# ConvFFN up projection as seven half-size products per pair of tiles, on one Trainium2 core

## The chip, the cores and the metric

The kernel runs on one core of a Trainium2 chip. The metric is the device time of one execution in microseconds (us): 802.35 us in the median of three runs (802.0 to 802.36). The engines of the core are called PE (TensorE, matrix multiply; PEld is its weight load), DVE (VectorE), ACT (ScalarE), POOL (GpSimd) and SP (SyncE, which here only issues DMA transfers). Each engine takes its instructions in the order in which they stand in its own queue, and waits on semaphores of the others.

## What is computed

One layer of a decoder trunk on a sequence of 512 tokens with 1024 features. A mixer of two gated branches comes first, then the ConvFFN, then a gated embedding and a last norm. The change concerns the ConvFFN, cut to its core here (D_FF is 2816):

```python
h = rmsnorm(x, ffn_norm)
up = h @ w_up                              # [512,1024] @ [1024, 5632]
conv = conv_b + sum(conv_w[k] * up_pad[:, k:k+T] for k in range(3))   # causal, width 3
a, b = conv[..., :2816], conv[..., 2816:]
x = x + (gelu(a) * b) @ w_down             # [512,2816] @ [2816, 1024]
```

All data is float32. The kernel splits every operand exactly into two float32r parts, high and low, and makes one product of three matmuls: high by high, high by low, low by high.

## The kernel before

Features lie on partitions, tokens on the free axis, in tiles of 128 x 512. `mm3` (L107 to L111) is one product of a 128 x 128 weight block with a 128 x 512 operand in three matmuls. `proj8` runs it over the eight k tiles of one output tile (24 matmuls into one PSUM bank).

Weights come as chunks of 128 x 1024 (512 KB). `chunk` (L53 to L61) issues one DMA on SP into `raw` (3 buffers), ACT casts `whi<-raw` (L59), DVE subtracts `wlo<-raw,whi` (L60). `take` hands out the chunks in a planned order and has each loaded two chunks ahead of its use.

The ConvFFN runs 22 times over a pair of f tiles, tile 2i (for a) and 2i+1 (for b). Per tile: `proj8`, then `conv` (L393 on): DVE multiplies the bank by the norm row R (L396), ACT scales (L398), DVE adds the two shifted terms (L399, L401). Then ACT takes gelu (L408), DVE multiplies a by b (L410), and `split` (L153, L154) stores the pair's h tile in two parts. After all 22 pairs the down projection runs over eight output tiles, 66 matmuls each, and `residual` adds each to x. The order of instructions on every engine is set by the tile framework's scheduler from program order and waits for buffers.

Of the kernel before, what the change touches and what calls it, by code (L numbers as in the profile page):

```python
# [36 lines left out]
def trunk(ctx, tc, xT, pT, wsT, par, bsp, w_p0, w_p1, w_v, w_u, w_ga, w_gb, w_pl,  # L37
# [15 lines left out]
    def chunk(src, cols=CW, keep=False, first=False):  # L53
        raw = wp.tile([P, CW], F32, tag="raw", name="raw", bufs=3)
# [39 lines left out]
    for f in range(KD):  # L94
        plan(w_o[f].rearrange(flat))
    for i in range(2 * KF):
        plan(w_up[i].rearrange(flat))
    DK = [(k0, min(8, KF - k0)) for k0 in range(0, KF, 8)]
    for f in range(KD):
        for k0, n in DK:  # L100
            plan(w_dn[f, :, k0:k0 + n, :].rearrange(flat), n * P)
# [91 lines left out]
    class Norm:
        """Sums squares of feature-major tiles; gives 1/rms by token and broadcast over partitions."""
# [19 lines left out]
        def row(self, r):  # L214
            """r[token] on every partition: ones times its diagonal blocks, in two exact parts."""
            rb = pst.tile([P, T], F32, tag="st", name="rb")
            dh = tmp.tile([P, PAD + T], F32R, tag="pad", name="dh", bufs=4)
            dl = tmp.tile([P, PAD + T], F32R, tag="pad", name="dl", bufs=4)
            for b in range(NT):
                c = slice(b * P, (b + 1) * P)  # L220
                V.tensor_scalar_mul(dh[:, c], ident, r[:, b:b + 1])
# [4 lines left out]
            return rb
# [18 lines left out]
    src, cols, kw = todo.pop(0)  # L245
    ready.append(chunk(src, cols, **kw))
# [123 lines left out]
    def residual(f, o, cg, nm=None):  # L370
        """x[f] += o; the next operand, and the sum of squares, with it."""
        xn = x[f]
        V.tensor_tensor(xn, o, xn, op=ALU.add)
        b = xgp.tile([P, 2, T], F32R, tag="xg", name="xg")
        split_into(b, xn, col(cg, f))
        if nm is not None:
            nm.add(xn)
        return b

# [1 line left out]
    nm = Norm()  # L381
    xg = [residual(f, proj8(m), C_FFN, nm) for f in range(KD)]

# [1 line left out]
    def up():  # L385
        return proj8(xg)

    up_o = [up()]
    r_tok = nm.token()
    up_o.append(up())  # L390
    R = nm.row_sb(r_tok)

    def conv(i):  # L393
        o = up_o[i] if i < len(up_o) else up()
        z = work("up")
        V.tensor_tensor(z, o, R, op=ALU.mult)  # L396
# [8 lines left out]
    h = []
    for i in range(KF):
        a = conv(2 * i)
        S.activation(a, a, AF.Gelu)  # L408
        b = conv(2 * i + 1)
        V.tensor_tensor(a, a, b, op=ALU.mult)  # L410
        h.append(split(a))
# [153 lines left out]
```

## Time and profile before

| | before |
|---|---|
| median of the runs | 802.35 us |
| profiled execution, span | 799.6 us |
| PE busy / DVE busy / ACT busy / POOL busy | 790.9 / 448.1 / 309.6 / 14.1 us |
| ConvFFN up stretch (373.27 to 614.08) | 240.8 us |
| down stretch (614.08 to 733.77) | 119.7 us |

The page gives the profiled execution as its span alone; the runs lie 2.75 us above it at the median, and that difference is taken as the time around the span. A matmul's duration in the trace holds its pipeline delay, so what one costs in a row of many is the distance from one start to the next.

### The profile page before, as it was taken

How to read it: one execution, taken by the hardware profiler on the slowest of the kernel's cores; microseconds unless marked ns; L12 is line 12 of the kernel's file. 1: busy time of each engine (PE TensorE's matmuls, PEld its weight loads, DVE VectorE, ACT ScalarE, POOL GpSimd, SP SyncE). 2: the span in 40 equal slices, each digit the busy share in tenths (PEclk: the TensorE clock that was granted, in tenths of full speed). 3: DMA queues.
4: the chain of work that ended last, by engine and by line, in shares of the span. 5: the costliest groups of instructions: out<-in, count | busy, mean ns of one | idle time of the engine just before them, and what ended most of it. 6: DMA issues, size and time to landing. Idle time of an engine off the chain costs nothing.

```text
span 799.6 us, 9000 instructions
## 1 busy us (share of the span) xinstructions
PE 790.9 (99%) x3566; PEld 657.6 (82%) x3566; DVE 448.1 (56%) x606; ACT 309.6 (39%) x421; POOL 14.1 (2%) x72
## 2 busy tenths in 40 slices
PE   9999999999999999999999999999999999999996
PEld 7888888888888888888888888888888888888885
DVE  7696353333665444555777777777777333235345
ACT  5235542223333232343444444444444222224534
POOL 0200000000000000000000000000000000000010
PEclk9999999999999999999999999999999999999999
DMA  7522322322222222223233233223233333325111
GB/s 251 202 82 78 131 93 92 105 94 91 81 93 90 90 96 105 100 86 105 80 106 105 82 103 105 85 101 106 83 101 118 98 94 100 98 99 173 64 53 54
DMA packets 24666, 81.44 MB, mean 102 GB/s; under 512 B 2864, under 2 KB 2992, under 8 KB 24624
## 3 DMA queue, kind: packets, MB, share of 16 engines
q1 hardware_dynamic: 23616, 78.65, 29.0%
q10 hardware_dynamic: 1008, 2.21, 0.9%
q8 instruction: 28, 0.46, 0.2%
q14 instruction: 14, 0.11, 0.0%
HBM read 78.75 MB, written 2.10 MB: 101 GB/s over the span
## 4 chain that ended last, share of the span: by engine, by line
PE 98%; DMA 0%; ACT 0%; DVE 0%; POOLq 0%; issue 0%; SPq 0%; ACTq 0%
PE mm L109 32%; PE mm L110 32%; PE mm L111 32%; PE mm L352 1%; PE mm L467 0%; DMA x<-in_xT 0%; PE ss L211 0%; ACT xg L156 0%; ACT ple L494 0%; POOLq L561 0%; ACT mm L487 0%; PE rb L224 0%; PE rb L225 0%; ACT mm L484 0%; DVE ple L485 0%
## 5 line engine op out<-in xcount | busy, mean ns | idle before, releaser
L59 ACT CAST whi<-raw 128x1024 fp32r<-128x1024 f32 (+1 forms) x141 | 146.0, 1038 | 312.7 <-PE mm L110 201.4
L109 PE MATMUL mm<-xg,whi 128*128 128x512 f32 x608 | 237.1, 391 | 0.5 <-ACT xg L156 0.5
L111 PE MATMUL mm<-xg,wlo 128*128 128x512 f32 x608 | 236.6, 389 | 0.0
L110 PE MATMUL mm<-xg,whi 128*128 128x512 f32 x608 | 236.6, 389 | 0.0
L60 DVE TENSOR_TENSOR wlo<-raw,whi 128x1024 fp32r<-128x1024 f32 (+1 forms) x148 | 174.4, 1180 | 105.4 <-ACT whi L59 103.2
L111 PE MATMUL mm<-blk,wlo 128*128 128x512 f32 x384 | 149.4, 389 | 0.0
L109 PE MATMUL mm<-blk,whi 128*128 128x512 f32 x384 | 149.4, 389 | 0.0
L110 PE MATMUL mm<-blk,whi 128*128 128x512 f32 x384 | 149.4, 389 | 0.0
L109 PEld LDWEIGHTS mm<-xg,whi 128*128 128x128 f32 x608 | 114.1, 188 | 24.0 <-ACT xg L156 0.7
L111 PEld LDWEIGHTS mm<-xg,wlo 128*128 128x128 f32 x608 | 114.2, 188 | 23.8
L110 PEld LDWEIGHTS mm<-xg,whi 128*128 128x128 f32 x608 | 114.1, 188 | 23.4
L111 PEld LDWEIGHTS mm<-blk,wlo 128*128 128x128 f32 x384 | 72.1, 188 | 15.0
L109 PEld LDWEIGHTS mm<-blk,whi 128*128 128x128 f32 x384 | 72.1, 188 | 15.0
L110 PEld LDWEIGHTS mm<-blk,whi 128*128 128x128 f32 x384 | 72.1, 188 | 14.9
L109 PE MATMUL mm<-whi,xg 128*128 128x512 f32 (+1 forms) x136 | 51.6, 379 | 0.0
L396 DVE TENSOR_TENSOR up<-mm,R 128x512 f32<-128x512 f32 x44 | 30.2, 687 | 38.1 <-PE mm L111 38.1
L111 PE MATMUL mm<-whi,xg 128*128 128x512 f32 (+1 forms) x136 | 51.2, 377 | 0.0
L110 PE MATMUL mm<-wlo,xg 128*128 128x512 f32 (+1 forms) x136 | 51.2, 377 | 0.0
L398 ACT ACTIVATE cc<-up,pr 128x512 f32<-128x512 f32 x44 | 35.7, 813 | 1.7 <-DVE up L396 1.4
L153 ACT CAST blk<-cc 128x512 fp32r<-128x512 f32 x22 | 13.7, 621 | 56.9 <-DVE cc L410 56.9
L332 DVE TENSOR_TENSOR gt<-mm,R 128x512 f32<-128x512 f32 x16 | 11.1, 692 | 42.5 <-PE mm L111 42.5
L401 DVE SCALAR_TENSOR_TENSOR cc<-up,pr,cc 128x510 f32<-128x510 f32 x44 | 33.0, 750 | 1.6
(104 smaller groups left out, 503.7 us busy)
## 6 DMA issues: line engine op xcount, KB each, us to landing
raw<-in_w_up SPq DMA_DIRECT2D x44, 512.0 KB, 3.2
raw<-in_w_dn SPq DMA_DIRECT2D x16, 512.0 KB, 3.5
raw<-in_w_v SPq DMA_DIRECT2D x8, 512.0 KB, 3.3
raw<-in_w_ga SPq DMA_DIRECT2D x8, 512.0 KB, 3.3
raw<-in_w_a SPq DMA_DIRECT2D x8, 512.0 KB, 3.2
raw<-in_w_u SPq DMA_DIRECT2D x8, 512.0 KB, 3.2
raw<-in_w_gb SPq DMA_DIRECT2D x8, 512.0 KB, 3.3
raw<-in_w_b SPq DMA_DIRECT2D x8, 512.0 KB, 3.2
```

The costliest lines, as they stand in the source:

```text
L59: (V.tensor_copy if first else S.copy)(hi[:, :cols], raw[:, :cols])
L60: V.tensor_tensor(lo[:, :cols], raw[:, :cols], hi[:, :cols].bitcast(F32), op=ALU.subtract)
L109: PE.matmul(o, wh, ah, start=first, stop=False)
L110: PE.matmul(o, wh, al, start=False, stop=False)
L111: PE.matmul(o, wl, ah, start=False, stop=last)
L153: S.copy(b[:, 0, :], src)
L332: V.tensor_tensor(gt, o, Rb, op=ALU.mult)
L352: PE.matmul(mx[:, n * P:(n + 1) * P], vt[n][:, f * P:(f + 1) * P], wsm[:, f, :], start=True, stop=True)
L396: V.tensor_tensor(z, o, R, op=ALU.mult)
L398: S.activation(cc, z, AF.Identity, scale=col(C_CW, 3 * i + 2), bias=col(C_CB, i))
L401: V.scalar_tensor_tensor(cc[:, 2:], z[:, :T - 2], col(C_CW, 3 * i), cc[:, 2:], op0=ALU.mult, op1=ALU.add)
```

## The change

Two output tiles of a pair, two halves of k (four k tiles each) and two halves of the tokens (256 each) make a 2 x 2 by 2 x 2 block product, which is formed by seven half-size products instead of eight (Strassen, Winograd's form). A product is now 4 k tiles x 3 matmuls of 128 x 256, and a pair has 84 of them in place of 48 of 128 x 512.

The operand sides (x times the norm's gain, and sums and differences of its halves) are made once, in `sides`, while the mixer's output projection runs. The weight sides are sums made per pair, in `sums`: `w1` is the plain chunk of the first tile; `ta` and `tb` hold the sums. Each of `ta` and `tb` is filled by one plain DMA from SP (256 KB), then one DMA issued by POOL that adds to what has landed, then one POOL addition (L108, L115); only then can ACT and DVE split it. The last chunk is the half `raw` that `two` loaded. So a pair splits 3.5 chunks in place of 2.

The down projection is cut into 22 steps of 24 matmuls: groups of four h tiles for two output tiles each (the last two steps: two h tiles, four output tiles), with each partial sum added to x. Seventeen steps stand between the products of pairs 5 to 21, five after the last pair.

The diff without its comment lines, cut to the core:

```diff
+NBLK = 26
+WB = 5
+HK = KD // 2
+FAHEAD = 3
+GS = 4
-    wp = ctx.enter_context(tc.tile_pool(name="wp", bufs=3))
+    wp = ctx.enter_context(tc.tile_pool(name="wp", bufs=WB))
-    xgp = ctx.enter_context(tc.tile_pool(name="xgp", bufs=8))
-    blk = ctx.enter_context(tc.tile_pool(name="blk", bufs=22))
+    blk = ctx.enter_context(tc.tile_pool(name="blk", bufs=NBLK))
...
+    def sums(f1, f2):
+        got = {}
+        top, bot = slice(0, HK), slice(HK, KD)
+        half = HK * P
+        flat = "p k f -> p (k f)"
+        def one():
+            got["1"] = raw_tile()
+            nc.sync.dma_start(got["1"], f1.rearrange(flat))
+            return parts(got["1"])
+        def two():
+            t = got["a"] = blk.tile([P, CW], F32, tag="blk", name="ta")
+            nc.sync.dma_start(t[:, :half], f1[:, top].rearrange(flat))
+            nc.gpsimd.dma_start(t[:, :half], f2[:, top].rearrange(flat), accum_op=ALU.add)
+            r = got["2"] = raw_tile()
+            nc.sync.dma_start(r[:, :half], f2[:, bot].rearrange(flat))
+            G.tensor_tensor(t[:, half:], t[:, :half], r[:, :half], op=ALU.add)
+            return parts(t)
+        def three():
+            t = blk.tile([P, CW], F32, tag="blk", name="tb")
+            nc.sync.dma_start(t[:, :half], f2[:, top].rearrange(flat))
+            nc.gpsimd.dma_start(t[:, :half], f2[:, bot].rearrange(flat), accum_op=ALU.add)
+            G.tensor_tensor(t[:, half:], got["a"][:, half:], got["1"][:, half:], op=ALU.add)
+            return parts(t)
+        return [one, two, three, lambda: parts(got["2"], half)]
...
+    def product(o, w, j, c, first=False):
+        for k in range(HK):
+            wh, wl = wslice(w, j * HK + k)
+            a = side(c, k)
+            for n, (p, q) in enumerate(((wh, a[:, 0]), (wh, a[:, 1]), (wl, a[:, 0]))):
+                PE.matmul(o, p, q, start=first and k == 0 and n == 0, stop=k == HK - 1 and n == 2, skip_group_check=True)
+        def begin(self):
+            self.w1 = take(FAHEAD)
+            self.p1 = bank()[:, :H]
+            self.b = seeded[self.i % 2][:, :H]
+            product(self.p1, self.w1, 0, 0, first=True)
+            S.copy(self.b, self.p1)
+        def middle(self):
+            wa = take(FAHEAD)
+            self.c = bank()[:, :H]
+            product(self.c, wa, 0, 3, first=True)
+            product(self.b, wa, 1, 4)
+            self.u = work("u").rearrange("p (a t) -> p a t", a=2)
+            S.copy(self.u[:, 0], self.b)
+            product(self.p1, self.w1, 1, 1)
+            V.tensor_tensor(self.z1[:, :H], self.p1, R[:, :H], op=ALU.mult)
+            self.wb = take(FAHEAD)
+            product(self.b, self.wb, 0, 5)
+            S.copy(self.u[:, 1], self.b)
+            V.tensor_tensor(self.z2[:, H:], self.c, self.u[:, 1], op=ALU.subtract)
+        def end(self):
+            product(self.b, self.wb, 1, 2)
+            V.tensor_tensor(self.z1[:, H:], self.b, R[:, H:], op=ALU.mult)
+            product(self.c, take(FAHEAD), 0, 6)
+            V.tensor_tensor(self.z2[:, :H], self.c, self.u[:, 0], op=ALU.subtract)
+            V.tensor_tensor(self.z2, self.z2, R, op=ALU.mult)
...
+    for i in range(KF):
+        pair.middle()
+        if order[i]:
+            down(order[i])
+        after = None
+        if i + 1 < KF:
+            after = Pair(i + 1)
+            after.begin()
+        h.append(pair.end())
+        pair = after
+    for step in steps:
+        down(step)
```

How the order of instructions moves is shown at two queues and, for one of them, the engine that it feeds. The SP queue of the kernel before, in the middle of the up stretch, holds one load per chunk, each waiting for DVE to have read the buffer's last content:

```order
L58 DMA raw_3471<-in_w_up 128x1024 [waits DMAHW2_49,DVE_49]
L58 DMA raw_3512<-in_w_up 128x1024 [waits DMAHW3_49,DVE_49]
L58 DMA raw_3550<-in_w_up 128x1024 [waits DMAHW4_49,DVE_49]
L58 DMA raw_3591<-in_w_up 128x1024 [waits DMAHW5_49,DVE_49]
L58 DMA raw_3629<-in_w_up 128x1024 [waits DMAHW6_49,DVE_49]
```

The SP queue of the changed kernel for one pair (pair 7) with a step of the down projection. `raw_3910` takes the buffer of `raw_3665`, the last chunk of pair 6 (a row of the DVE queue below); `ta_3835` and `tb_3875` are pair 7's sums:

```order
L99 DMA raw_3771<-in_w_up 128x1024 [waits DMAHW4_49,Pool_49]
L107 DMA raw_3838<-in_w_up 128x512 [waits DMAHW6_49,DMAHW1_49,DVE_49]
L62 DMA raw_3910<-in_w_dn 128x512 [waits DMAHW5_49,DVE_49,Activation_49]
L104 DMA ta_3835<-in_w_up 128x512 [waits DMASW0_49]
L113 DMA tb_3875<-in_w_up 128x512 [waits DMASW1_49]
L62 DMA raw_3910<-in_w_dn 128x512 [waits DMAHW7_49]
L99 DMA raw_3944<-in_w_up 128x1024 [waits DMAHW2_49,DMAHW0_49,Pool_49]
```

One load per chunk has become six issues per pair, and the loads of the sums stand behind a load that waits for DVE's last subtraction of the pair before. The POOL queue, which has no instruction in the up stretch before but one small one of the norm, now holds for each pair, here 6 and 7:

```order
L105 DMA ta_3662<-in_w_up 128x512 [waits DMAHW7_49,DMASW5_49,DVE_49]
L114 DMA tb_3702<-in_w_up 128x512 [waits DMAHW0_49,DVE_49]
L108 TENSOR_TENSOR ta_3662<-ta_3662,raw_3665 128x512 [waits DMAHW5_49,DMASW4_49]
L115 TENSOR_TENSOR tb_3702<-ta_3662,raw_3598 128x512 [waits DMAHW4_49,Pool_49]
L105 DMA ta_3835<-in_w_up 128x512 [waits DMAHW5_49,DVE_49]
L114 DMA tb_3875<-in_w_up 128x512 [waits DMASW7_49,DMAHW6_49,DMASW1_49,DVE_49]
L108 TENSOR_TENSOR ta_3835<-ta_3835,raw_3838 128x512 [waits DMAHW3_49,DMASW6_49]
L115 TENSOR_TENSOR tb_3875<-ta_3835,raw_3771 128x512 [waits DMAHW2_49,Pool_49]
```

Each is new: two adding transfers and two additions per pair. The DVE queue of the kernel before, for about one pair:

```order
L396 TENSOR_TENSOR up_3780<-mm_3755,R_2861 128x512 [waits PE_49]
L60 TENSOR_TENSOR wlo_3789<-raw_3787,whi_3788 128x1024 [waits DMAHW5_49,Activation_49]
L399 SCALAR_TENSOR_TENSOR cc_3782<-up_3780,pr_82,cc_3782 128x511 [waits Activation_49]
L401 SCALAR_TENSOR_TENSOR cc_3782<-up_3780,pr_82,cc_3782 128x510 [waits DVE_49]
L396 TENSOR_TENSOR up_3818<-mm_3793,R_2861 128x512 [waits PE_49]
L60 TENSOR_TENSOR wlo_3830<-raw_3828,whi_3829 128x1024 [waits DMAHW6_49,Activation_49]
L399 SCALAR_TENSOR_TENSOR cc_3820<-up_3818,pr_82,cc_3820 128x511 [waits Activation_49]
```

The DVE queue of the changed kernel, from the subtraction of pair 6's `ta` to that of its last chunk (`raw_3665`):

```order
L74 TENSOR_TENSOR wlo_3669<-ta_3662,whi_3668 128x1024 [waits DMASW4_49,Activation_49]
L74 TENSOR_TENSOR wlo_3707<-tb_3702,whi_3706 128x1024 [waits DMASW5_49,Activation_49]
L74 TENSOR_TENSOR wlo_3741<-raw_3737,whi_3740 128x1024 [waits DMAHW6_49,DMAHW1_49,Activation_49]
L520 TENSOR_TENSOR z2_3528<-z2_3528,R_2905 128x512 [waits DVE_49]
L532 SCALAR_TENSOR_TENSOR cc_3758<-z1_3527,pr_79,cc_3758 128x510
L74 TENSOR_TENSOR wlo_3774<-raw_3771,whi_3773 128x1024 [waits DMAHW2_49,Activation_49]
L530 SCALAR_TENSOR_TENSOR cc_3763<-z2_3528,pr_79,cc_3763 128x511 [waits Activation_49]
L509 TENSOR_TENSOR z1_3700<-mm_3710,R_2905 128x256 [waits PE_49]
L532 SCALAR_TENSOR_TENSOR cc_3763<-z2_3528,pr_79,cc_3763 128x510 [waits DVE_49]
L74 TENSOR_TENSOR wlo_3818<-raw_3665,whi_3817 128x512 [waits DMAHW5_49]
```

Before, one subtraction of a chunk stands between the steps of a tile's convolution; now the five subtractions of a pair stand nearly together, with steps of two convolutions between them, and ten instructions separate the first from the last.

## Rows read from the trace of the kernel before

**Rows 1.** Busy time, share of the span and instructions of each engine, from the page.
```profile
PE 790.9 (99%) x3566; PEld 657.6 (82%) x3566; DVE 448.1 (56%) x606; ACT 309.6 (39%) x421; POOL 14.1 (2%) x72
```

**Rows 2.** The chain that ended last, by engine, from the page.
```profile
PE 98%; DMA 0%; ACT 0%; DVE 0%; POOLq 0%; issue 0%; SPq 0%; ACTq 0%
```

**Rows 3.** Busy time by stretch (up, down): PE, PEld, DVE, ACT, POOL, clock, DMA.
```profile
373.20:614.10 240.90, 240.90 (x1069) 199.58 (x1068) 175.31 (x227) 108.90 (x135) 1.01 (x1) 1.00 0.28 96
614.10:734.00 119.90, 119.90 (x530) 99.31 (x529) 44.70 (x49) 34.03 (x38) 0.00 (x0) 1.00 0.34 106
```

**Rows 4.** PE in time (start, duration): first up matmul, first and last of 528 down.
```profile
373.27 0.39 PE L109 MATMUL mm<-xg,whi 128*128 128x512 f32 x1
...
614.08 0.39 PE L109 MATMUL mm<-blk,whi 128*128 128x512 f32 x1
...
733.53 0.40 PE L111 MATMUL mm<-blk,wlo 128*128 128x512 f32 x1
```

**Rows 5.** PE in time: first and last of 48 half-width matmuls, last token block.
```profile
786.57 0.28 PE L109 MATMUL mm<-whi,xg 128*128 128x256 f32 x1
...
792.20 0.28 PE L111 MATMUL mm<-whi,xg 128*128 128x256 f32 x1
```

**Rows 6.** Groups of DVE by line and form (busy us, mean ns, idle before).
```profile
L60 DVE TENSOR_TENSOR wlo<-raw,whi 128x1024 fp32r<-128x1024 f32 x132 | 161.2, 1224 | 102.2 <-ACT whi L59 100.0
L401 DVE SCALAR_TENSOR_TENSOR cc<-up,pr,cc 128x510 f32<-128x510 f32 x44 | 33.0, 750 | 1.6
L410 DVE TENSOR_TENSOR cc<-cc 128x512 f32<-128x512 f32 x22 | 15.2, 692 | 0.7
L488 DVE TENSOR_TENSOR ple<-xt,gB 128x256 f32<-128x256 f32 x2 | 0.8, 425 | 0.1
```

**Rows 7.** DVE in time, up stretch and last block.
```profile
430.18 1.23 DVE L60 TENSOR_TENSOR wlo<-raw,whi 128x1024 fp32r<-128x1024 f32 x1 [0.17 <-ACT whi L59]
431.32 0.74 DVE L399 SCALAR_TENSOR_TENSOR cc<-up,pr,cc 128x511 f32<-128x511 f32 x1
432.10 0.75 DVE L401 SCALAR_TENSOR_TENSOR cc<-up,pr,cc 128x510 f32<-128x510 f32 x1
...
434.26 0.69 DVE L154 TENSOR_TENSOR blk<-cc,blk 128x512 fp32r<-128x512 f32 x1 [0.69 <-ACT blk L153]
434.87 0.68 DVE L396 TENSOR_TENSOR up<-mm,R 128x512 f32<-128x512 f32 x1
```

**Rows 8.** Groups of ACT by line and form.
```profile
L59 ACT CAST whi<-raw 128x1024 fp32r<-128x1024 f32 x132 | 138.7, 1053 | 290.1 <-PE mm L110 179.5 <-issue 88.7 <-PE mm L111 12.3
L398 ACT ACTIVATE cc<-up,pr 128x512 f32<-128x512 f32 x44 | 35.7, 813 | 1.7 <-DVE up L396 1.4
L153 ACT CAST blk<-cc 128x512 fp32r<-128x512 f32 x22 | 13.7, 621 | 56.9 <-DVE cc L410 56.9
```

**Rows 9.** DMA issues: count, KB each, median us from issue to landing.
```profile
raw<-in_w_up SPq DMA_DIRECT2D x44, 512.0 KB, 3.2
...
raw<-in_w_p SPq DMA_DIRECT2D x8, 256.0 KB, 3.4
x<-in_xT SPq DMA_DIRECT2D x8, 256.0 KB, 3.9
...
out<-ple SPq DMA_DIRECT2D x8, 256.0 KB, 2.2
```

**Rows 10.** Groups of POOL by line and form.
```profile
L451 POOL TENSOR_TENSOR fr<-fms,neghalf 128x1 f32<-128x1 f32 x8 | 4.4, 563 | 409.9 <-DVE fms L449 409.9
L190 POOL TENSOR_TENSOR rt<-ms,neghalf 128x4 f32<-128x4 f32 x3 | 4.0, 1332 | 312.9 <-DVE ms L188 312.9
...
L270 POOL TENSOR_SCALAR_AFFINE_SELECT wsm<-wsm 128x1024 f32<-128x1024 f32 x1 | 1.6, 1596 | 24.0 <-DMA wsm<-in_wsT 24.0
```

**Rows 11.** SP's own queue in time: one issue at the program's start.
```profile
2.17 0.43 SPq L58 DMA_DIRECT2D raw<-in_w_p  x1
```

**Rows 12.** Busy time by stretch after PE's last matmul (columns as in rows 3).
```profile
793.00:795.00 2.00, 0.00 (x0) 0.00 (x0) 1.43 (x4) 0.51 (x2) 0.24 (x1) 1.00 0.00 0
795.00:797.00 2.00, 0.00 (x0) 0.00 (x0) 0.49 (x1) 0.72 (x1) 0.30 (x1) 0.79 0.15 59
797.00:799.60 2.60, 0.00 (x0) 0.00 (x0) 0.00 (x0) 0.00 (x0) 0.00 (x0) 0.50 0.41 156
```

More of the change, by code (lines that the diff above doesn't have):

```diff
@@ L93, in trunk @@
         plan(w_b[f].rearrange(flat))
[L94 to L101, printed above, removed]
+    for k in range(HK):
+        for f in (k, HK + k):
+            plan(w_o[f].rearrange(flat))
+    steps = []
+    for g0 in range(0, KF, GS):
+        n = min(GS, KF - g0)
+        fs = CW // (n * P)
+        steps += [(g0, n, tuple(range(f0, f0 + fs)), g0 + n) for f0 in range(0, KD, fs)]
+    order = []
+    units = [sums(w_up[2 * i], w_up[2 * i + 1]) for i in range(KF)]
+    todo.append(units[0][0])
+    for i in range(KF):
+        down = steps.pop(0) if steps and steps[0][3] < i else None
+        order.append(down)
+        todo += units[i][1:3]
+        if down:
+            g0, n, fs, _ = down
+            plan(*[w_dn[f, :, g0:g0 + n, :].rearrange(flat) for f in fs])
+        if i + 1 < KF:
+            todo.append(units[i + 1][0])
+        todo.append(units[i][3])
+    for g0, n, fs, _ in steps:
+        plan(*[w_dn[f, :, g0:g0 + n, :].rearrange(flat) for f in fs])
     for k in range(2):
@@ L243, in load @@
         x.append(xt)
[L245 to L246 removed]
+    ready.append(todo.pop(0)())
     load(0)
@@ L368, in trunk @@
         m.append(split(gt))
[L370 to L378, printed above, removed]
-    nm = Norm()
[L382 to L396, printed above, removed]
+    stage.close()
+    ps = stage.enter_context(tc.tile_pool(name="ps2", bufs=5, space=PSUM))
+    psb = stage.enter_context(tc.tile_pool(name="psb", bufs=1, space=PSUM))
+    nm = Norm()
+    def half_tile(name):
+        return blk.tile([P, 2, 2, H], F32R, tag="blk", name=name)
+    a11 = [half_tile("a11") for _ in range(HK // 2)]
+    cmb = [[half_tile("cmb") for _ in range(3)] for _ in range(HK)]
@@ new lines, in sides @@
+    def sides(k, s1, s2):
+        E = V if k == HK - 1 else G
+        d = work("d").rearrange("p (a t) -> p a t", a=2)
+        e = work("e").rearrange("p (a t) -> p a t", a=2)
+        E.tensor_tensor(d[:, 0], s1[:, H:], s2[:, H:], op=ALU.subtract)
+        E.tensor_tensor(d[:, 1], d[:, 0], s1[:, :H], op=ALU.subtract)
+        E.tensor_tensor(e[:, 0], s1[:, :H], s1[:, H:], op=ALU.subtract)
+        E.tensor_tensor(e[:, 1], s2[:, :H], d[:, 1], op=ALU.add)
+        o = a11[k // 2][:, k % 2]
+        S.copy(o[:, 0], s1[:, :H])
+        V.tensor_tensor(o[:, 1], s1[:, :H], o[:, 0].bitcast(F32), op=ALU.subtract)
+        for t, src in zip(cmb[k], (s2.rearrange("p (a t) -> p a t", a=2), d, e)):
+            S.copy(t[:, :, 0], src)
+            V.tensor_tensor(t[:, :, 1], src, t[:, :, 0].bitcast(F32), op=ALU.subtract)
@@ new lines, in side @@
+    def side(c, k):
+        return a11[k // 2][:, k % 2] if c == 0 else cmb[k][(c - 1) // 2][:, (c - 1) % 2]
+    for k in range(HK):
+        sc = []
+        for f in (k, HK + k):
+            o = proj8(m)
+            V.tensor_tensor(x[f], o, x[f], op=ALU.add)
+            sx = work("sx")
+            S.activation(sx, x[f], AF.Copy, scale=col(C_FFN, f))
+            nm.add(x[f])
+            sc.append(sx)
+        sides(k, *sc)
+    seeded = [psb.tile([P, T], F32, tag=f"sd{n}", name="sd") for n in range(2)]
@@ new lines, in trunk @@
+    for t in seeded:
+        for c in range(2):
+            PE.matmul(t[:, c * P:(c + 1) * P], ones_r, ones_r, start=c == 0, stop=True, skip_group_check=True)
+    def product(o, w, j, c, first=False):
+        for k in range(HK):
+            wh, wl = wslice(w, j * HK + k)
+            a = side(c, k)
+            for n, (p, q) in enumerate(((wh, a[:, 0]), (wh, a[:, 1]), (wl, a[:, 0]))):
+                PE.matmul(o, p, q, start=first and k == 0 and n == 0, stop=k == HK - 1 and n == 2, skip_group_check=True)
@@ new lines, in trunk, with __init__ @@
+    class Pair:
+        def __init__(self, i):
+            self.i = i
+            self.z1, self.z2 = work("z1"), work("z2")
+        def begin(self):
[23 more added lines that the diff above has]
+            V.tensor_tensor(self.z2, self.z2, R, op=ALU.mult)
+            a = conv(2 * self.i, self.z1)
+            S.activation(a, a, AF.Gelu)
+            b = conv(2 * self.i + 1, self.z2)
+            V.tensor_tensor(a, a, b, op=ALU.mult)
+            return split(a)
@@ L405, in trunk, with down @@
     h = []
-    for i in range(KF):
[L407 to L411, printed above, removed]
+    xg2 = [None] * KD
+    def down(step):
+        g0, n, fs, end = step
+        w = take(FAHEAD)
+        for q, f in enumerate(fs):
+            o = bank()
+            for k in range(n):
+                mm3(o, wslice(w, q * n + k), act(h[g0 + k]), k == 0, k == n - 1)
+            V.tensor_tensor(x[f], o, x[f], op=ALU.add)
+            if end == KF:
+                xg2[f] = split(x[f], col(C_PLE, f))
+    pair = Pair(0)
+    pair.begin()
+    r_tok = nm.token()
+    R = nm.row_sb(r_tok)
+    for i in range(KF):
+        pair.middle()
+        if order[i]:
+            down(order[i])
+        after = None
+        if i + 1 < KF:
+            after = Pair(i + 1)
[4 more added lines that the diff above has]
+        down(step)
+    stage.close()
+    ps = stage.enter_context(tc.tile_pool(name="ps3", bufs=7, space=PSUM))
     pp = []
```

31 lines of the change are left out of this document (17 added, 14 removed).

## Prediction

> **What bounds the kernel now.** I read the busy line first: PE is busy 99% of the span, DVE 56%, ACT 39%, POOL 2% [rows 1]. The chain of waits agrees, with 98% on PE [rows 2]. By stretch, PE is busy through the whole up and down parts at a granted clock of 1.00, DVE is busy for 175.3 of 240.9 us and 44.7 of 119.9, POOL not at all, and the DMA engines for about a third [rows 3]. So the ConvFFN now lasts as long as its matmuls. In the timeline of PE the down part's 528 matmuls start from 614.08 to 733.53, 119.45/527 = 0.2267 us apart [rows 4]. The 1056 of the up part at that distance make 239.4 us; the stretch is 240.8, the rest being the norm's small matmuls.
>
> **PE: what the change saves.** After it a pair issues 84 matmuls of 128 x 256 in place of 48 of 128 x 512. Half-width matmuls stand in the last token block: 48 of them from 786.57 to 792.20, 5.63/47 = 0.120 us apart [rows 5], which is 53% of a full one, not 50%. Up: 22 x 84 x 0.120 = 221.8 us. The down part keeps its 528 matmuls, 119.7 us. PE saves 239.4 - 221.8 = 17.6 us, and no more. Per pair PE then has 84 x 0.120 = 10.08 us; with a down step (24 x 0.2267 = 5.44) 15.52.
>
> **DVE and ACT.** Starts on DVE give distances of 1.14 us for a full subtraction, 0.78 for a shifted term, 0.61 for a product of 512 columns [rows 7]; half a subtraction costs 0.69, a 256-column one 0.43 [rows 6]. A pair now needs 3 x 1.14 + 0.69 for 3.5 chunks, 4 x 0.43 + 0.61 for z1 and z2, 4 x 0.78 of convolution, 0.61 + 0.69 for h: 10.9 us; with a down step another subtraction and two additions to x, 13.2. That is under 15.52 where a step stands, and 0.8 over 10.08 in the five pairs (0 to 4) without one, by sums of average costs alone. ACT's casts (1.05), scalings (0.81) and small copies (0.62 for 512 columns) [rows 8] stay near 9 us per pair. Neither sets the pace of pairs with a step by its sum.
>
> **What the loading of the sums adds.** In the orders of SP, POOL and DVE I find a closed round per pair. (a) DVE subtracts `ta` of pair n, and nine instructions later the last chunk of pair n. (b) SP's load of w_dn takes that last chunk's raw buffer, so SP waits there for that subtraction. (c) The plain load of `ta` for pair n+1 stands behind it on SP, although its own buffer is free. (d) POOL's adding DMA waits for that landing, (e) POOL's addition (L108) waits for the adding DMA, (f) ACT's cast waits for the addition, and (g) DVE's subtraction of `ta` of pair n+1 waits for the cast, which closes the round. One pair cannot take less than one round, whatever PE does; loading three chunks ahead doesn't help, as the round goes through the queues. The terms:
> - DVE from `ta` to the last chunk: ten instructions, four full subtractions, z2 by R, three shifted terms, a half of z1 and half a subtraction: 4 x 1.14 + 0.61 + 3 x 0.78 + 0.43 + 0.69 = 8.63 us [rows 6, 7].
> - ACT's cast 1.05 and its handover 0.04: 1.09 [rows 8].
> - SP's issue of the load in front: 0.43 [rows 11].
> - The landing of `ta` behind 256 KB of w_dn, so 512 KB in all: 3.2 us, the row of w_up; from 2.2 to 3.9 over the 256 KB rows [rows 9].
> - The adding DMA: no row has one. Nearest is the plain 256 KB load, 3.4 us [rows 9], plus the shortest instruction of POOL's, 0.56 [rows 10], for POOL's part in issuing it: 4.0, which I take. Below it is bounded by the shortest 256 KB transfer, 2.2; above by reading and writing the target one after the other, twice 3.9 = 7.8.
> - POOL's addition of 128 x 512: POOL has none. I take the 1.33 us of its longest tensor_tensor, rounded to 1.3; bounds are DVE's 0.69 for that form [rows 6] and POOL's 1.6 for 1024 columns [rows 10].
>
> The round: 8.63 + 1.09 + 0.43 + 3.2 + 4.0 + 1.3 = 18.65 us, against PE's 15.52: 3.13 us are not hidden, in each of the 16 pairs 6 to 21, 50.1 us. With all low ends it is 15.24 and hidden; with all high ends 23.45, 7.9 us too long.
>
> On the adding DMA the Trainium skill ("DMA: Bandwidth & Descriptors", the section on the anatomy of a DMA on GpSimd's path) gives a fixed 2.0 us plus the bytes at 436 GB/s, an estimate of 2.6 us for 256 KB. No run here shows such a DMA; the plain loads, 2.2 to 3.9 us for the same bytes [rows 9], hold that value. By it the round is 17.25 us and the kernel's time about 817; the sum here goes by the 4.0 of the rows.
>
> **Pairs 0 to 4.** Without a w_dn load the load in front of `ta` takes its buffer by turns. For pairs 3 and 5 it is the load in (c) of the last half chunk, released by POOL's addition of `tb`; the round is 1.3 + 0.43 + 3.2 + 4.0 + 1.3 = 10.2 us against PE's 10.08, 0.15 each. For pair 4 it is `w1`'s, released by the last subtraction: cast 1.09, then 3 x 1.14 + 0.61 + 0.69 = 4.72, then 0.43 + 8.5 = 14.7, so 4.7. Together 5.0 us (about 20 with the high ends, none with the low ones).
>
> **Start.** The operand sides are made beside the mixer's output projection. For three of the four k POOL and DVE do it behind PE; for the last one DVE's addition to x (0.69, nearest row), ACT's scaling by the gain (0.72 as the mean of 0.81 and 0.62), two sums (0.43 each) and the casts stand before the first product that needs them, but the first product (12 matmuls, 1.44 us) and the norm's matmuls need only the plain half. I take 1.1 us. The 2 x 22 additions to x in partial sums lie on DVE within its 13.2 us, and their price on PE is nothing, as five banks turn over.
>
> **Sum.** 799.6 - 17.6 + 50.1 + 5.0 + 1.1 = 838.2 us of span; with the 2.75 us by which the runs' median lies above the profiled span, 841 us, against 802.35.
>
> **Rivals.**
> 1. The round is hidden: landing, adding DMA and addition together take under 15.52 - 8.63 - 1.09 - 0.43 = 5.4 us where I take 8.5. For it: 2.2 + 2.2 + 0.69 = 5.1 at the low ends, and the DMA engines are two thirds idle [rows 3]. Against it: 512 KB alone have not landed faster than 3.2 us at the median [rows 9], which leaves 2.2 for an adding DMA and an addition on POOL. Then PE bounds: 799.6 - 17.6 + 1.1 + 2.75 = 785.9; `ta`'s cast stands on ACT behind a scaling of 0.81 in the 17 pairs with a step, half of it lost each time is 7 us: 793. Faster.
> 2. DVE becomes the bound, since POOL's additions hold it up. No row shows the two engines together in this stretch (POOL does nothing there [rows 3]). If each addition of 1.3 us stops DVE for its whole length, DVE has 10.9 + 2.6 = 13.5 us in pairs 0 to 4 and 15.8 in the others: 5 x 3.4 + 17 x 0.3 = 22 us, and with the round hidden otherwise 785.9 + 22 = 808. Slower; it decides from 2.5 us of stall per pair on, where 5 x (0.8 + 2.5) + 17 x (13.2 + 2.5 - 15.52) has used up the 16.5 us that PE saves. The Trainium skill ("SBUF — State Buffer", the section on who interferes with whom) says that a DVE instruction with two SBUF inputs and a GpSimd one that reads SBUF exclude each other, the later one waiting in full; every subtraction here is such a one.
> 3. The adding DMA is much longer, 6 to 7.8 us. Each microsecond more costs 16 in the pairs with a step and about 3 before: at 6 us 841 + 38 = 879, at 7.8 about 913; with all high ends at once 799.6 - 17.6 + 127 + 20 + 1.1 + 2.75 = 933. For it speaks only that it must read its target as well.
> 4. Waits on PE lower its clock. The granted clock was 0.79 and 0.50 in the two stretches after 795.00, PE's last matmul having started at 792.20 [rows 5, 12]. The forecast's 3.1 us of waiting per pair is shorter than what stands there before the fall, so I give this no share of its own; it would add to the forecast.
>
> **How the numbers follow.** The forecast's case, the round as the bound with terms near those taken, gets 0.64 and reaches from 815 (the adding DMA at 2.6) to 870 (at 5.5). The hidden round gets 0.14, DVE as the bound 0.08, the long adding DMA 0.14. The range of 8 in 10, from 793 to 885, leaves out the lower half of the hidden round (0.07) and the long adding DMA above 6.2 us (0.1). What a measurement of this kernel can tell from no change is about 0.2%, 1.6 us. Faster has the hidden round's lower part and a little of the bound by DVE: 0.15; between 800.7 and 804.0 lies 0.03; slower has the rest, 0.82.
>
> **What would show it.** Right, if pairs 6 to 21 begin about 18.7 us apart, PE's idle time there stands before the products with `ta` and is ended by DVE's `wlo` or ACT's `whi`, SP's w_dn load issues as the last subtraction ends, and the chain of waits runs through SP, DMA, POOL, ACT and DVE in each pair. The PE saving is right if 84 half-width matmuls in a row lie 0.120 us apart. The adding DMA and POOL's addition show their length in their own rows. Wrong, if PE is busy over 97% of the up part, or if DVE is never idle there, or if the wait before `ta` is ended by a buffer of another kind.

## The result, and the profile after

The changed kernel takes 877.15 us (median of 4 runs, 875.46 to 877.93) against 802.25 us: ratio 1.0932, 95% interval 1.0917 to 1.0948. It is slower, by 74.9 us. The forecast was slower by 39, at 841 us.

The page's busy line and chain by engine answer to [rows 1] and [rows 2]:

```profile
PE 812.3 (93%) x4362; PEld 705.2 (80%) x4362; DVE 543.4 (62%) x766; ACT 368.1 (42%) x545; POOL 124.2 (14%) x172
...
PE 63%; DVE 10%; DMA 9%; issue 7%; POOL 6%; ACT 3%; SPq 1%; POOLq 0%; ACTq 0%; DVEq 0%
```

PE has fallen from 98% of the chain to 63%, and DVE, DMA and POOL have come into it: the mark of a chain that goes through several engines in turn. By stretch (columns as in rows 3), the first five pairs and then pairs 5 to 21 answer to [rows 3]:

```profile
375.00:480.00 105.00, 85.33 (x587) 80.37 (x586) 76.04 (x108) 50.66 (x75) 32.26 (x28) 0.90 0.46 116
480.00:761.00 281.00, 248.93 (x1568) 225.48 (x1567) 192.57 (x265) 119.17 (x175) 61.90 (x57) 0.95 0.47 123
```

No engine is busy all the time, where PE was before, and TensorE's granted clock is 0.90 and 0.95 where it was 1.00.

One turn of the round, from pair to pair, in the timeline of all engines (start, duration, engine, line; in brackets the idle time before and its releaser):

```profile
514.74 1.66 DVE L74 TENSOR_TENSOR wlo<-ta,whi 128x1024 fp32r<-128x1024 f32 x1 [0.22 <-ACT whi L73]
...
522.75 0.69 DVE L74 TENSOR_TENSOR wlo<-raw,whi 128x512 fp32r<-128x512 f32 x1
...
523.50 0.33 SPq L62 DMA_DIRECT2D raw<-in_w_dn  x1
...
523.88 0.63 SPq L104 DMA_DIRECT2D ta<-in_w_up  x1
...
528.01 0.86 POOL L105 DMA_DIRECT2D ta<-in_w_up  x1 [12.69 <-DMA ta<-in_w_up]
...
531.80 1.26 POOL L108 TENSOR_TENSOR ta<-ta,raw 128x512 f32<-128x512 f32 x1 [1.82 <-DMA ta<-in_w_up]
...
533.09 1.04 ACT L73 CAST whi<-ta 128x1024 fp32r<-128x1024 f32 x1 [2.18 <-POOL ta L108]
...
534.16 1.32 DVE L74 TENSOR_TENSOR wlo<-ta,whi 128x1024 fp32r<-128x1024 f32 x1 [2.13 <-ACT whi L73]
534.18 0.50 PE L487 MATMUL mm<-cmb,whi 128*128 128x256 f32 x2 [2.07 <-ACT whi L73]
```

The reader sees the seven links in order: DVE's `ta`, its last chunk (ends 523.44), SP's w_dn load at 523.50, the plain load of `ta` behind it, POOL's adding DMA, POOL's addition, ACT's cast, DVE's next `ta`, 19.42 us after the first. PE had waited 2.07 us for the end of that cast. The 16 turns of pairs 5 to 21 stand beside the forecast's terms, each as the mean over their rows:

| link of the round | forecast | measured |
|---|---|---|
| DVE `ta` to the last chunk, and SP's issue in front | 9.06 | 9.07 |
| issue of `ta`'s plain load to POOL's adding DMA | 3.2 | 3.79 |
| POOL's adding DMA to POOL's addition | 4.0 | 4.02 |
| POOL's addition | 1.3 | 1.29 |
| ACT's cast and handover | 1.09 | 1.11 |
| sum | 18.65 | 19.28 |

The first pairs, by DVE's subtractions of `ta` in its timeline, and the last for the mean:

```profile
376.47 1.34 DVE L74 TENSOR_TENSOR wlo<-ta,whi 128x1024 fp32r<-128x1024 f32 x1 [2.26 <-ACT whi L73]
...
394.04 1.21 DVE L74 TENSOR_TENSOR wlo<-ta,whi 128x1024 fp32r<-128x1024 f32 x1
...
413.77 1.21 DVE L74 TENSOR_TENSOR wlo<-ta,whi 128x1024 fp32r<-128x1024 f32 x1
...
427.11 1.22 DVE L74 TENSOR_TENSOR wlo<-ta,whi 128x1024 fp32r<-128x1024 f32 x1
...
443.76 1.65 DVE L74 TENSOR_TENSOR wlo<-ta,whi 128x1024 fp32r<-128x1024 f32 x1 [0.56 <-ACT whi L73]
...
458.56 1.21 DVE L74 TENSOR_TENSOR wlo<-ta,whi 128x1024 fp32r<-128x1024 f32 x1
...
766.98 1.32 DVE L74 TENSOR_TENSOR wlo<-ta,whi 128x1024 fp32r<-128x1024 f32 x1 [1.96 <-ACT whi L73]
```

Pairs 5 to 21: (766.98 - 458.56)/16 = 19.28 us each. Pairs 0 to 4, each from its own `ta` to the next pair's: 17.6, 19.7, 13.3, 16.7 and 14.8, together 82.1 us, where PE needs 50.4. So against a kernel bound by PE the later pairs lose 16 x (19.28 - 15.52) = 60.1 us and the first five 31.7; less the 17.6 that PE saves, that is 74.2 of the 76.6 us by which the span grew.

### The profile page after: what moved, and what is told of

The parts are those of the page before. It is cut to its first block, busy times and chain, and to the rows that moved or that the text cites. A ratio compares the mean times of both kernels' runs of the same rounds, so it can differ in the third digit from the quotient of the medians.

```text
span 876.2 us, 11251 instructions
## 1 busy us (share of the span) xinstructions
PE 812.3 (93%) x4362; PEld 705.2 (80%) x4362; DVE 543.4 (62%) x766; ACT 368.1 (42%) x545; POOL 124.2 (14%) x172
## 4 chain that ended last, share of the span: by engine, by line
PE 63%; DVE 10%; DMA 9%; issue 7%; POOL 6%; ACT 3%; SPq 1%; POOLq 0%; ACTq 0%; DVEq 0%
PE mm L169 18%; PE mm L170 17%; PE mm L171 17%; DMA tb<-in_w_up 6%; DVE wlo L74 5%; PE sd L487 4%; PE mm L487 4%; POOL ta L108 2%; ACT whi L73 2%; DMA ta<-in_w_up 2%; POOL tb L115 2%; POOL tb L114 2%; DVE cc L532 2%; DMA raw<-in_w_up 1%; DVE cc L530 1%
## 5 line engine op out<-in xcount | busy, mean ns | idle before, releaser
L487 PE MATMUL mm<-cmb,whi 128*128 128x256 f32 x528 | 111.4, 308 | 35.2 <-ACT whi L73 35.2
L487 PEld LDWEIGHTS mm<-cmb,whi 128*128 128x128 f32 x528 | 91.4, 212 | 38.8 <-ACT whi L73 38.8
L487 PE MATMUL sd<-cmb,whi 128*128 128x256 f32 x528 | 107.6, 300 | 5.0 <-ACT u L507 2.2
L169 PE MATMUL mm<-xg,whi 128*128 128x512 f32 x256 | 100.5, 395 | 0.0
L170 PE MATMUL mm<-xg,whi 128*128 128x512 f32 x256 | 99.7, 389 | 0.0
L171 PE MATMUL mm<-xg,wlo 128*128 128x512 f32 x256 | 99.6, 389 | 0.0
L487 PEld LDWEIGHTS sd<-cmb,whi 128*128 128x128 f32 x528 | 90.3, 208 | 10.2 <-ACT u L507 5.8
L487 PE MATMUL mm<-cmb,wlo 128*128 128x256 f32 x264 | 83.1, 317 | 10.0 <-DVE wlo L74 9.9
L487 PE MATMUL sd<-cmb,wlo 128*128 128x256 f32 x264 | 79.1, 300 | 0.0
L169 PEld LDWEIGHTS mm<-xg,whi 128*128 128x128 f32 x256 | 48.4, 190 | 9.8
L171 PEld LDWEIGHTS mm<-xg,wlo 128*128 128x128 f32 x256 | 48.0, 188 | 10.1
L170 PEld LDWEIGHTS mm<-xg,whi 128*128 128x128 f32 x256 | 48.1, 188 | 9.6
```

The costliest lines, as they stand in the source:

```text
L169: PE.matmul(o, wh, ah, start=first, stop=False)
L170: PE.matmul(o, wh, al, start=False, stop=False)
L171: PE.matmul(o, wl, ah, start=False, stop=last)
L487: PE.matmul(o, p, q, start=first and k == 0 and n == 0, stop=k == HK - 1 and n == 2, skip_group_check=True)
```

## The experiments

The theory on trial is the round through SP's order. The rivals are the adding DMA or the buffers as such, POOL and DVE in each other's way, the cut of the down projection, and PE's clock.

**Own buffers for the sums.** The tiles `ta` and `tb` get a ring of three, out of the 26.

```diff
-NBLK = 26
+NBLK = 23
-            t = got["a"] = blk.tile([P, CW], F32, tag="blk", name="ta")
+            t = got["a"] = blk.tile([P, CW], F32, tag="tab", name="ta", bufs=3)
-            t = blk.tile([P, CW], F32, tag="blk", name="tb")
+            t = blk.tile([P, CW], F32, tag="tab", name="tb", bufs=3)
```

> The sums' tiles ta and tb get three buffers of their own, taken from the 26 that they shared with the rest (23 are left); no work changes. In the order of SP their plain loads then stand ahead of the load of w_dn that waits for DVE's last subtraction, where in the changed kernel they stood behind it. Theory of the round through SP: the 19.3 us from one pair's sum to the next (pairs 5 to 21) fall to 15.5 to 16.5 us, the first five pairs from 16.4 to about 12, and the time from 877 to 800 to 825 us. Rival, DVE held up by POOL's additions: as many additions run, so over 865 us. Rival, PE's lowered clock as a cause of its own: it can only go if the waits go, so this run falls as well, but matmuls in a row would still be slow.

Measured: 809.84 us, ratio to before 1.0098 (1.0083 to 1.0113). The same transfers and additions, 67 us less. SP's order is now the other way round: the load of `ta` goes out about 10 us ahead of the w_dn loads. DVE's timeline shows the distance of the later pairs:

```profile
517.28 0.33 SPq L104 DMA_DIRECT2D ta<-in_w_up  x1
...
527.47 0.80 SPq L62 DMA_DIRECT2D raw<-in_w_dn  x2
```

```profile
435.19 1.22 DVE L74 TENSOR_TENSOR wlo<-ta,whi 128x1024 fp32r<-128x1024 f32 x1
...
684.16 1.21 DVE L74 TENSOR_TENSOR wlo<-ta,whi 128x1024 fp32r<-128x1024 f32 x1
```

(684.16 - 435.19)/16 = 15.56 us for pairs 5 to 21, about PE's own 15.52; pairs 1 to 4 fell from 16.1 to 11.4 us each, while pair 0 rose from 17.6 to 22.4, as its `ta` was split 9.4 us earlier. From 470 to 690 PE is busy throughout, at a granted clock of 1.00:

```profile
470.00:690.00 220.00, 220.00 (x1532) 206.58 (x1531) 190.86 (x254) 115.59 (x170) 68.02 (x55) 1.00 0.57 148
```

So the order in which SP's loads stood is the cause of the loss in the later pairs; more buffers without another order give nothing back (the run with four raw buffers, below). The ConvFFN's last matmul began at 731.59 us, but the program still ended at 807.2. DVE's timeline shows what came at the end, after PE's last matmul, which started at 792.03:

```profile
794.01 1.28 DVE L640 TENSOR_TENSOR ple<-xt,gB 128x512 f32<-128x512 f32 x2
795.21 0.88 DVE L648 TENSOR_SCALAR ple<-ple,fr 128x512 f32<-128x512 f32 x2
...
799.99 1.03 DVE L640 TENSOR_TENSOR ple<-xt,gB 128x512 f32<-128x512 f32 x2
```

All products with `gB` stand in a row: with three shared buffers fewer, `gB` found its place late.

**Without the adding DMAs.** The sums lack the second tile's part that these would add.

```diff
-            nc.gpsimd.dma_start(t[:, :half], f2[:, top].rearrange(flat), accum_op=ALU.add)
...
-            nc.gpsimd.dma_start(t[:, :half], f2[:, bot].rearrange(flat), accum_op=ALU.add)
```

> The two DMAs per pair that add the second tile's weights to ta and tb are left out (the sums lack that part); SP's order and waits, POOL's additions and all other work stay. Theory of the round: it loses the 3.8 us of the adding DMA and POOL's issue of it, 19.3 becomes about 15.5, where PE's 15.52 takes over: 805 to 825 us. Rival, POOL's additions contend with DVE: they all stay, so over 865 us. Rival, the landing of the plain loads alone is what hurts: about 850.

Measured: 811.35 us, 1.0126 (1.0107 to 1.0144). From pair 6 on the pairs lie 15.5 to 16.3 us apart; pairs 1 to 4 take 14.1 each. Taking one link of 4.0 us out of the round is enough, with SP's order as it was: the round has then about PE's length.

**Four raw buffers.**

```diff
-        return wp.tile([P, CW], F32, tag="raw", name="raw", bufs=3)
+        return wp.tile([P, CW], F32, tag="raw", name="raw", bufs=4)
...
-                self.acc = tmp.tile([P, T], F32, tag="acc", name="acc", bufs=2)
+                self.acc = tmp.tile([P, T], F32, tag="acc", name="acc", bufs=1)
```

> Four raw buffers in place of three (and one buffer in place of two for the norm's sum, for the room; nothing else uses the second during the ConvFFN). The w_dn load no longer takes the buffer of the pair's last chunk, but by the order of SP the w1 load of the next pair but one then takes it and still stands ahead of ta's load. Theory of the round through SP's order: it stays closed, 18.5 to 20 us per pair, 865 to 890 us. Rival, too few raw buffers as such: with a third more the time falls by at least half of what was lost, under 840 us.

Measured: 885.32 us, 1.1042 (1.1026 to 1.1059), 19.37 us per turn. More buffers alone don't help: another load (w1 in place of w_dn) waits for the same subtraction and still stands ahead of `ta` on SP:

```profile
529.45 0.69 DVE L74 TENSOR_TENSOR wlo<-raw,whi 128x512 fp32r<-128x512 f32 x1
...
530.22 0.33 SPq L99 DMA_DIRECT2D raw<-in_w_up  x1
530.59 0.43 SPq L104 DMA_DIRECT2D ta<-in_w_up  x1
```

Which load stands behind which decides, not their number of buffers.

**The down projection's cut alone.** The kernel before, with its steps between the pairs.

```diff
+        if order[i]:
+            down(order[i])
+    for step in steps:
+        down(step)
...
-    xg2 = []
-    for f in range(KD):
-        ch = [(take(), n) for _, n in DK]
-        xg2.append(residual(f, project(ch, h), C_PLE))
```

> The kernel before with only its down projection cut into the same 22 steps, seventeen of them between the pairs, with the partial sums added to x; the up projection is the one of before (48 matmuls of 512 columns per pair, no sums). Theory: PE has the same matmuls and five or more banks turn over, so 800 to 806 us, as before. Rival, the steps between the pairs cost by themselves (DVE's additions, w_dn loads between the others): over 815 us.

Measured: 801.63 us, 1.0000 (0.9991 to 1.0009). By itself that half of the change costs and gives nothing, so the loss needs the loading of the sums. In the changed kernel the two meet: the w_dn loads of the steps are what `ta`'s load stands behind.

**Whole loads.** No adding DMA and no load of a sum; POOL makes four additions per pair.

```diff
-            nc.sync.dma_start(t[:, :half], f1[:, top].rearrange(flat))
-            nc.gpsimd.dma_start(t[:, :half], f2[:, top].rearrange(flat), accum_op=ALU.add)
-            nc.sync.dma_start(r[:, :half], f2[:, bot].rearrange(flat))
-            G.tensor_tensor(t[:, half:], t[:, :half], r[:, :half], op=ALU.add)
+            nc.sync.dma_start(r, f2.rearrange(flat))
+            G.tensor_tensor(t[:, :half], got["1"][:, :half], r[:, :half], op=ALU.add)
+            G.tensor_tensor(t[:, half:], t[:, :half], r[:, half:], op=ALU.add)
...
-            nc.sync.dma_start(t[:, :half], f2[:, top].rearrange(flat))
-            nc.gpsimd.dma_start(t[:, :half], f2[:, bot].rearrange(flat), accum_op=ALU.add)
+            G.tensor_tensor(t[:, :half], r[:, :half], r[:, half:], op=ALU.add)
```

> Both tiles' weights of a pair come as two plain loads of 512 KB into raw buffers (in place of five loads and adding DMAs of 256 KB and one of 512), and all four half sums are made by POOL from them; no DMA adds, and no load of a sum stands on SP. 26 shared buffers as in the changed kernel. Theory of the round: SP's loads now hold only raw buffers, the round is gone, PE sets the pace: 15.5 us per pair with a step, 11 to 12 without, 790 to 800 us, faster than before (802) by 0.3 to 1.5%. Rival, POOL and DVE in each other's way: POOL has twice the additions (5.2 us per pair), DVE's subtractions rise from 1.23 us to over 1.5 and the time is over 806. Rival, the PE saving is eaten elsewhere: 800 to 806.

Measured: 826.86 us, 1.0307 (1.0293 to 1.0321). My theory failed here and the rival held. The round is gone and the later pairs take 15.84 us each, but pairs 0 and 1 take 21.7 and 17.2 us and pairs 2 to 4 15.5 in place of 11 to 12. The timeline of POOL and DVE shows why, first in pair 3, then in a pair with a step:

```profile
430.73 2.29 POOL L110 TENSOR_TENSOR tb<-raw 128x512 f32<-128x512 f32 x1
...
431.78 2.32 DVE L74 TENSOR_TENSOR wlo<-tb,whi 128x1024 fp32r<-128x1024 f32 x1
...
432.98 2.27 POOL L104 TENSOR_TENSOR ta<-ta,raw 128x512 f32<-128x512 f32 x1
...
434.02 2.31 DVE L74 TENSOR_TENSOR wlo<-raw,whi 128x1024 fp32r<-128x1024 f32 x1
```

```profile
565.84 1.73 POOL L110 TENSOR_TENSOR tb<-raw 128x512 f32<-128x512 f32 x1
...
566.35 1.77 DVE L74 TENSOR_TENSOR wlo<-raw,whi 128x512 fp32r<-128x512 f32 x1
...
567.54 1.74 POOL L104 TENSOR_TENSOR ta<-ta,raw 128x512 f32<-128x512 f32 x1
...
568.05 1.77 DVE L520 TENSOR_TENSOR cc<-cc 128x512 f32<-128x512 f32 x1
```

In pair 3 DVE's full subtractions take 2.3 us in place of 1.22 and POOL's additions 2.3 in place of 1.29. With a step DVE's half subtraction and its product of 512 columns, 0.69 us each before [rows 6], take 1.77, and POOL's additions 1.73. Their starts alternate, in the second stretch 1.70 us apart on either engine: while both have work, neither goes at its own pace.

**z2's product on POOL too.**

```diff
-            V.tensor_tensor(self.z2, self.z2, R, op=ALU.mult)
+            G.tensor_tensor(self.z2, self.z2, R, op=ALU.mult)
```

> As the run with whole loads, and the product of z2 with the norm's row goes from DVE to POOL, which takes 0.6 us per pair off DVE. Theory: in the first five pairs DVE's 10.9 us against PE's 10.08 are the bound, so these get 0.5 us shorter each, 1 to 3 us in all, and nothing changes after them. Rival, POOL is slow and its result late: 0 to 5 us longer than the run with whole loads.

Measured: 844.33 us, 1.0535 (1.0521 to 1.0550). Both expectations missed: 17.5 us longer, over three times the upper end of the rival's. A fifth instruction on POOL took 2.17 us, the pairs with a step 17.1 us each, and DVE's shifted terms rose to 1.14 and 1.38 us. DVE's busy time rose from 591.4 to 610.1 us although it had 22 products fewer: work moved from DVE to POOL made DVE slower.

**Own buffers, tail mended.**

```diff
-    ple = [blk.tile([P, D], F32, tag="blk", name="ple") for _ in range(NT)]
+    ple = [blk.tile([P, D], F32, tag="tab" if b < 2 else "blk", name="ple", bufs=3 if b < 2 else None) for b in range(NT)]
...
-    gB = blk.tile([P, D], F32, tag="blk", name="gB")
+    gB = blk.tile([P, D], F32, tag="tab", name="gB", bufs=3)
```

> As the run with own buffers for the sums, and the tail's gB and the first two ple tiles use those three buffers after the ConvFFN, so that the tail has as many as before. In the own-buffers run the ConvFFN's last matmul ended 1.8 us earlier than in the kernel before, but the tail took 74.3 us from there in place of 65.8, with DVE's last products in a row after PE was done. Theory: the tail goes back to 66 us and the time to 799 to 803 us (0 to 0.4% faster than before). Rival, something else late in the tail: it stays at 806 to 811.

Measured: 801.10 us, 0.9995 (0.9982 to 1.0009), the same as the kernel before. The time fell by 8.7 us and the tail, from the ConvFFN's last matmul to the end, from 75.7 to 67.5 us in the profiles, as expected. Both runs lose about 5 us in the mixer, long before the ConvFFN: PE's 200th matmul starts at 51.6 and 51.7 us where the changed kernel has 46.7, and PE waits 3.6 us at 37 us for DVE's `dh`, part of a norm. Why stays open.

**The same, with DVE's additions.** Both lines on top of the one before it.

```diff
-            G.tensor_tensor(t[:, half:], t[:, :half], r[:, :half], op=ALU.add)
+            V.tensor_tensor(t[:, half:], t[:, :half], r[:, :half], op=ALU.add)
-            G.tensor_tensor(t[:, half:], got["a"][:, half:], got["1"][:, half:], op=ALU.add)
+            V.tensor_tensor(t[:, half:], got["a"][:, half:], got["1"][:, half:], op=ALU.add)
```

> As the run with own buffers and the tail mended, with the two additions per pair made by DVE in place of POOL. Theory that POOL and DVE stop each other: DVE gets 1.2 us per pair of its own and loses 0.3 to 1.0 us of stalls, its instructions at 0.68 us each stay at 0.68; the time is within 4 us of that run either way. Rival, POOL's additions cost DVE nothing: 0 to 6 us longer, by 1.2 us in the pairs where DVE bounds.

Measured: 796.61 us, 0.9935 (0.9922 to 0.9948): faster than both kernels, 4.5 us below the run before it, a little more than the 4 expected. DVE took on two instructions per pair and the time fell. Its half subtraction is back at 0.68 us from 1.07 and its second shifted term at 0.74 from 0.95 (means from 460 to 680). From the first matmul of the up projection to the last of the down projection the run takes 347.2 us against 360.3 before, 13 us less; about 5 of them are lost again in the mixer, as in the run before it. The page's busy line, and two turns of DVE's timeline:

```profile
PE 781.0 (98%) x4362; PEld 684.1 (86%) x4362; DVE 553.6 (70%) x810; ACT 368.6 (46%) x545; POOL 63.3 (8%) x128
```

```profile
556.60 1.22 DVE L74 TENSOR_TENSOR wlo<-ta,whi 128x1024 fp32r<-128x1024 f32 x1
...
572.15 1.22 DVE L74 TENSOR_TENSOR wlo<-ta,whi 128x1024 fp32r<-128x1024 f32 x1
```

15.55 us: this is what PE's 84 half-width matmuls and 24 full ones were reckoned at (15.52) from [rows 4, 5].

**Whole loads, DVE's additions.** As the run with whole loads, `V` for `G` in all four additions.

> As the run with whole loads (827 us), with all four additions per pair made by DVE in place of POOL. There DVE's half subtraction took 1.69 us and its product of the two tiles 1.69 in place of 0.69 and 0.68, each beside an addition of POOL's. Theory that the two engines stop each other: DVE gets 2.4 us per pair of its own and loses 4 of stalls, the first five pairs fall from 15.5 to about 13.3 us, the others to 15.6, the time to 805 to 818 us. Rival, DVE is simply slower there for another reason: DVE at 13.3 + 2.4 us per pair, over 840 us.

Measured: 803.73 us, 1.0020 (1.0011 to 1.0029), 23 us below the run with the same four additions on POOL. Pairs 2 to 4 fell from 15.5 to 12.6 us. Pair 3 on DVE:

```profile
416.30 1.22 DVE L74 TENSOR_TENSOR wlo<-ta,whi 128x1024 fp32r<-128x1024 f32 x1
...
418.90 1.21 DVE L74 TENSOR_TENSOR wlo<-raw,whi 128x1024 fp32r<-128x1024 f32 x1
```

Full subtractions are back at 1.22 us from the 2.31 of pair 3 there, half ones at 0.68 from the 1.77 with a step. That settles the rival of the slower DVE: it was POOL's company that cost.

## Why the prediction was right, and where its size was off

The direction and the mechanism were right: the round through SP's order set the pace, as the forecast had it. The size was half of what came, 39 us for 75, and that the range still held 877 us is in part luck: the forecast's case was let end at 870, and the room up to 885 was kept for the long adding DMA, which didn't come.

- **PE's saving** was right. Pairs with a step take 15.55 us once nothing else holds them (the last own-buffers run), against 15.52.
- **The round** was right in its place, its order and, but for one link, its price. Four of its five rows in the table are within 0.02 us of the forecast. The row that is off is the one that I called "the landing of `ta` behind 256 KB of w_dn": 3.79 us to POOL's adding DMA in place of 3.2. The landing itself took 3.23 us in the mean of the 16 turns, as I had it. What the sum lacked is the way from the landing to the start of POOL's adding DMA (527.46 to 528.01 in the turn shown), 0.56 us in the mean, which I had put at nothing while I gave ACT's handover a term. The whole round is 0.63 us longer than forecast, and 0.63 x 16 = 10 us. That DVE's row agrees to 0.01 us is luck in part: its shifted terms stand 0.66 us apart where I took 0.78, and the subtraction of `ta` costs 1.46 in the mean where I took 1.14.
- **Pairs 0 to 4** are the step that failed in size: they lose 31.7 us in place of 5.0, 26.7 of the 38 us by which the forecast of the span (838.2 for 876.2) was short. I had one pair (4) with the long round through the last subtraction and put pairs 1 and 2 at nothing. Pair 2's `ta` took that same round, 19.7 us after pair 1's. For pair 1 I had misread a row: I wrote that POOL does nothing in the up stretch, while [rows 3] has one instruction of 1.01 us there, the norm's. In the changed kernel POOL's queue shows that small instruction ahead of the adding DMAs:

```profile
382.58 1.52 POOL L250 TENSOR_TENSOR rt<-ms,neghalf 128x4 f32<-128x4 f32 x1 [5.86 <-DVE ms L248]
384.07 0.90 POOL L114 DMA_DIRECT2D tb<-in_w_up  x1
384.70 1.16 POOL L105 DMA_DIRECT2D ta<-in_w_up  x1
385.24 1.51 POOL L114 DMA_DIRECT2D tb<-in_w_up  x1
390.02 1.32 POOL L108 TENSOR_TENSOR ta<-ta,raw 128x512 f32<-128x512 f32 x1 [3.27 <-DMA ta<-in_w_up]
```

  POOL waited 5.86 us for the norm with an adding DMA behind, and three of them then ran at once, 5.3 us from `ta`'s issue to its addition. That way took 5.08 for pair 3 and 5.66 for pair 5 (448.77 to 454.43), where I had 4.0. That SP's order is the cause in pairs 1 to 4 together is shown by the own-buffers run (16.1 to 11.4 us each); what the norm's wait alone cost was not tried.
- **Rival 1**, the hidden round, didn't come. The three links that it needs under 5.4 us took 9.1.
- **Rival 2**, DVE stopped by POOL, was not the bound of this kernel: while the round holds everything, POOL adds mostly when DVE is idle; the subtraction of `ta` beside the addition of `tb` shows it (1.66 us at 514.74), and seven of the shifted terms. But it is what comes next once the round is gone, as the runs with whole loads show. My price of 2.6 us per pair for two additions was too high: between the run with own buffers and the tail mended and the one with DVE's additions, the half subtraction and the four shifted terms of a pair differ by about 1.0 us together. The Trainium skill ("SBUF — State Buffer", who interferes with whom) says that a DVE instruction with two SBUF inputs and a reading one of GpSimd exclude each other in full; the trace nearly agrees, with 1.70 us a turn on both, where the instructions alone stand 0.61 (DVE) and 1.24 us (POOL) apart, together 1.85.
- **Rival 3**, the long adding DMA, fell: 4.02 us. The estimate of 2.6 us from the figures of the Trainium skill ("DMA: Bandwidth & Descriptors", anatomy on GpSimd's path) is below it; from POOL's issue to the use of the data no turn has under 3.73.
- **Rival 4**, the clock, I had put aside because the waits are short. That was wrong as a statement on the clock (below). It can have cost little in the later pairs: the round's links add up to their distance without PE, and in 13 of the 16 turns DVE is never idle between `ta` and the last chunk. For the first pairs it is open, as the runs that lost the waits got the clock back with them.
- **The five steps after the last pair, the start and the partial sums** were priced about right: 2.4 us are left over for them together, where I had 1.1. The cut of the down projection cost nothing by itself.

## What to carry to other kernels

When a change adds loads to a queue, write down for each what it stands behind, and close the loop through the engines: a load whose buffer is free can still wait a whole turn behind one whose buffer is not, and reading ahead doesn't help. Buffers of their own for the late-used loads changed the order and gave back 67 us of 75, a buffer more in the common ring gave nothing. Before handing additions to an idle POOL, look at whether DVE reads two SBUF operands beside them: here the busier engine was the cheaper place. And reckon the first turns of a loop like the others, not as an average.

## What the runs showed of the hardware

POOL and DVE took turns at 1.70 us per instruction where each alone takes 1.29 and 0.69 for the same 512 columns. Moving one product of 0.6 us per pair from DVE to POOL cost 17.5 us in all.

TensorE's granted clock fell after waits of about 2 us: between 480 and 770 us it fell with each of the ten waits of 1.84 to 2.59 us, at its end or within 2.1 us of it. Its timeline before and after the wait of 2.07 us at 534.18, and two stretches (columns as in rows 3):

```profile
528.71 0.40 PE L487 MATMUL sd<-cmb,whi 128*128 128x256 f32 x2
528.95 0.28 PE L487 MATMUL sd<-cmb,wlo 128*128 128x256 f32 x1
529.07 0.40 PE L487 MATMUL sd<-cmb,whi 128*128 128x256 f32 x2
...
535.92 0.63 PE L487 MATMUL mm<-cmb,whi 128*128 128x256 f32 x2
536.34 0.41 PE L487 MATMUL mm<-cmb,wlo 128*128 128x256 f32 x1
536.56 0.63 PE L487 MATMUL mm<-cmb,whi 128*128 128x256 f32 x2
```

```profile
528.00:531.00 3.00, 3.00 (x28) 3.00 (x27) 0.48 (x2) 1.17 (x2) 1.72 (x2) 1.00 0.62 128
536.00:538.00 2.00, 2.00 (x11) 2.00 (x11) 2.00 (x3) 0.62 (x2) 0.00 (x0) 0.50 0.52 195
```

Three matmuls take 0.36 us ahead of it, at a granted clock of 1.00 (2.4 GHz), and 0.64 after, at 0.50 (1.2 GHz). By 539.05 three take 0.36 again. Over the stretch from 480 to 761 the granted clock is 0.95.

An adding DMA of 256 KB cost POOL's queue 0.86 us and was ready 3.7 to 4.3 us after its issue in 14 of 16 turns; the plain load of `ta` ahead of it landed 3.2 us after its own. POOL began that DMA 0.54 to 0.57 us after the landing that it waited for, but its addition 0.07 to 0.08 us after the adding DMA's.
